# Intermediates of a two-block transformer kernel kept in their PSUM banks, and one bias vector moved

## The chip, the cores and the metric

The kernel runs on one core of a Trainium2 chip. The metric is the time of one execution on the device in microseconds, the median of three runs. The core has five engines with queues of their own: TensorE (PE, matrix products), VectorE (DVE) and ScalarE (ACT) for elementwise work, GpSimd (POOL), and SyncE (SP), which here only issues transfers. An engine takes its instructions in order and waits on semaphores. Operands lie in SBUF; TensorE writes its products into PSUM, eight banks of 128 partitions by 512 float32, which DVE and ACT can read and write.

## What is computed

256 rows of 1024 channels go through two blocks. Shortened:

```python
# block 1
h    = layer_norm(x)
proj = h @ w_in + b_in                  # qa ka va qb kb vb, gates ga gb
y_na, y_swa = neighbourhood(...) @ w_branch_na, windowed(...) @ w_branch_swa
mixed = sigmoid(ga) * y_na + sigmoid(gb) * y_swa
h = layer_norm(alpha * h + mixed @ w_out + b_out)
u = square(relu(h @ w_ff1 + b_ff1))
h = layer_norm(alpha * h + u @ w_ff2 + b_ff2)
# block 2, two layers: pooling mixer, then windowed attention
for layer in range(2):
    m = mixer(rms_norm(x))
    x = x + rms_norm(m, mix_post_g)
    c = conv3(rms_norm(x) @ w_in) + conv_b          # causal, depthwise
    gate, val = split(c)
    x = x + rms_norm((gelu(gate) * val) @ w_out, ffn_post_g)
```

## The kernel before

The 256 rows are two tiles `t` of 128. Every product is carried in a rounded high part and a low part of both operands: `hi*hi + hi*lo + lo*hi`, three matmuls each. Activations are split by ScalarE (high part: a rounding copy) and VectorE (low part: source minus high part); `split_out` (L337) does it for `oh/ol`, `uh/ul`, `ah/al`.

Weights stream in slices of 512 KB. SyncE issues the transfer into `wraw`, ScalarE writes `whi` (L131), VectorE or GpSimd writes `wlo` (L141, function `low`, whose `eng` says which). A slice's next transfer waits until `wlo` is done. `W.pump(n, eng)` prepares slices, `W.take` hands one to TensorE. All of it stands in program order on the engines' queues, without a planner: code order is the order of the work.

PSUM banks come in two rotations of four, `bank_a` and `bank_b`. Units of two output halves (`unit_a`, L371) compute 128 columns by 256 rows per half into a `bank_a`; `epi(m, o)` is what is done with half `m`, and what it returns runs after the slices of that step are pumped. `Tm` is used where the second row tile is late: `run(t)` computes transposed rows, `finish(u, epi)` transposes them back. `Acc` holds the four `bank_b` of a 256x1024 sum; `acc.tail` finishes tile 0 first, so that its norm runs beside the products of tile 1.

The places that the change touches:

- Branch sums, L762 to L779. Four units; per half: gate times branch plus the other branch's product (L770, L772, VectorE), high part (L775, ScalarE), low part (L777, VectorE). Behind each half a slice's `wlo` goes to VectorE (m = 0) or GpSimd (m = 1).
- First norms, `post_ln` (L793): residual sum, statistics, centring (L279), output (L284), on VectorE. Tile 0 runs inside `acc.tail`, tile 1 after it, beside `tm.run(0)`.
- Between `to_fm(h1[1])` and `tm.run(1)`: two VectorE instructions (L907) that turn `h1` into `alpha*h1 + bff2`. `bff2` is a 512 KB broadcast transfer on GpSimd's queue (`vec`, L217).
- Feed-forward: units 3 to 15, each followed by two slices of the second product. Its norms are `a_stats`, `a_centre`, `a_norm`.
- Mixer, L1030 on: the residual product (`resid_g`, L327), sums of squares on ScalarE (`sq_half`, L302), `resid_add` (L331). A product `junk` tile in SBUF joins the two.
- Gated convolution (`conv_ffn`, L1074): per unit half a ScalarE read of the bank (L1085) and two taps on VectorE (L1086, L1088); with m = 1 gelu (L1092, ScalarE), gate product (L1093, VectorE), split. Units 0 to 2 are finished from `Tm` into `bank_b` between the first three of units 3 to 21; while u < 6 GpSimd takes the `wlo` of the pump.

## Time and profile before

| what | value |
|---|---|
| runs | 896.19, 897.50, 894.68 us; median 896.19 |
| profiled execution | 895.49 us, of which span 893.7 us |
| mean granted TensorE clock | 0.984 |
| TensorE busy | 847.2 us (95% of the span) |
| VectorE, ScalarE, GpSimd busy | 630.2 us (71%), 492.2 us (55%), 238.3 us (27%) |
| chain that ended last | PE 66%, DVE 14%, issue 6%, ACT 6%, DMA 5%, POOL 2% |

The profile is of one execution. TensorE is busy in all but some tens of microseconds, so the places that count are those where it stands still and those where its matmuls are spaced wider than elsewhere. A row of a timeline gives the start in microseconds, the duration, the engine, the line of the kernel, the operation, what is written and read, and in brackets the idle time before it with the instruction that ended it. Overlapping starts are the engine's pipeline. For TensorE the distance from one start to the next is the pace, not the printed duration.

### The profile page before, as it was taken

The page shows a single profiled execution, that of the slowest core. Times are in us where ns is not written, and L with a number is a line of the kernel's source. Part 1 is how long each engine was busy: PE and PEld are TensorE (multiplying, and loading weights), DVE is VectorE, ACT ScalarE, POOL GpSimd, SP SyncE. Part 2 cuts the span into 40 slices and gives each one's busy share as a digit, 9 for nine tenths or more (in the row PEclk, how much of TensorE's full clock was granted, in tenths as well). Part 3 has the DMA queues.
Part 4 walks back from the last instruction along what each step waited for, and adds up shares of the span by engine and source line. Part 5 has one row for each costly group of instructions (what it writes and reads, how often), then busy time and mean ns, then how long its engine had stood idle before and what let it go on. Part 6 is the DMA issues. An engine that isn't in the chain of part 4 may idle for free.

```text
span 893.7 us, 15200 instructions
## 1 busy us (share of the span) xinstructions
PE 847.2 (95%) x5872; PEld 764.6 (86%) x5872; DVE 630.2 (71%) x1019; ACT 492.2 (55%) x905; POOL 238.3 (27%) x196
## 2 busy tenths in 40 slices
PE   6999999889899999998999999999999899999997
PEld 5988899768798999788989999988776899999995
DVE  5466754877747755777689877765796678977772
ACT  4555755433535655444666555465786466655551
POOL 4161040323999000343240000046721224000000
PEclk9999999989899999998999999999999999999999
DMA  8683354337635865523447656544152354765531
GB/s 316 201 276 117 134 189 140 120 104 237 224 102 184 278 246 189 184 100 118 165 124 253 217 185 213 179 129 130 59 198 99 142 189 149 261 227 186 179 133 47
DMA packets 43897, 154.61 MB, mean 173 GB/s; under 512 B 5009, under 2 KB 5905, under 8 KB 43826
## 3 DMA queue, kind: packets, MB, share of 16 engines
q1 hardware_dynamic: 41616, 146.90, 48.5%
q0 software_dynamic: 1632, 5.93, 2.1%
q8 instruction: 46, 0.75, 0.3%
q10 hardware_dynamic: 578, 0.82, 0.3%
q14 instruction: 25, 0.20, 0.1%
HBM read 152.58 MB, written 1.05 MB: 172 GB/s over the span
## 4 chain that ended last, share of the span: by engine, by line
PE 66%; DVE 14%; issue 6%; ACT 6%; DMA 5%; POOL 2%; DVEq 0%; POOLq 0%; SPq 0%; ACTq 0%
PE bank_a L369 35%; PE bank_b L369 23%; DVE wlo L141 4%; DMA wraw<-wts_dram 4%; PE bank_a L424 3%; ACT whi L131 2%; DVE p L1262 1%; DVE p L698 1%; ACT p L1274 1%; PE bank_a L720 1%; POOL wlo L141 1%; PE bank_b L709 1%; DVE X L331 1%; DMA v<-bvec_dram 1%; PE bank_b L657 1%
## 5 line engine op out<-in xcount | busy, mean ns | idle before, releaser
L141 DVE TENSOR_TENSOR wlo<-wraw,whi 128x1024 fp32r<-128x1024 f32 x225 | 287.1, 1304 | 78.9 <-ACT whi L131 73.3
L369 PE MATMUL bank_a<-xh,whi 128*128 128x256 f32 x1056 | 297.3, 282 | 4.1 <-DVE cv L1088 3.9
L369 PE MATMUL bank_a<-xh,wlo 128*128 128x256 f32 x1056 | 294.3, 279 | 0.7 <-DVE wlo L141 0.5
L369 PE MATMUL bank_a<-xl,whi 128*128 128x256 f32 x1056 | 294.1, 278 | 0.0
L131 ACT ACTIVATE whi<-wraw 128x1024 fp32r<-128x1024 f32 x261 | 265.5, 1050 | 41.3 <-DMA wraw<-wts_dram 35.0
L369 PEld LDWEIGHTS bank_a<-xh,whi 128*128 128x128 f32 x1056 | 200.0, 189 | 9.2 <-ACT whi L131 4.6
L369 PEld LDWEIGHTS bank_a<-xl,whi 128*128 128x128 f32 x1056 | 200.1, 189 | 1.8
L369 PEld LDWEIGHTS bank_a<-xh,wlo 128*128 128x128 f32 x1056 | 200.0, 189 | 1.3 <-DVE wlo L141 1.0
L141 POOL TENSOR_TENSOR wlo<-wraw,whi 128x1024 fp32r<-128x1024 f32 x36 | 93.6, 2617 | 173.2 <-ACT whi L131 74.8
L1085 ACT ACTIVATE cv<-bank_a,cols 128x256 f32<-128x256 f32 x76 | 41.9, 559 | 78.5 <-PE bank_a L369 78.5
L266 POOL TENSOR_TENSOR rstd<-ve,neghalf 128x1 f32<-128x1 f32 x22 | 13.5, 612 | 232.1 <-DVE ve L307 189.8
L369 PE MATMUL bank_b<-wlo,ah 128*128 128x512 f32 x176 | 69.3, 394 | 0.0
L369 PE MATMUL bank_b<-whi,al 128*128 128x512 f32 x176 | 69.0, 392 | 0.0
L369 PE MATMUL bank_b<-whi,ah 128*128 128x512 f32 x176 | 68.5, 389 | 0.0
L1086 DVE SCALAR_TENSOR_TENSOR cv<-bank_a,cols,cv 128x255 f32<-128x255 f32 x76 | 36.5, 481 | 44.5 <-ACT cv L1085 44.3
L869 POOL TENSOR_SCALAR wraw<-wraw,cols 128x256 f32<-128x256 f32 x28 | 29.5, 1074 | 122.9 <-DVE cv L1086 117.4
L369 PE MATMUL bank_b<-whi,uh 128*128 128x512 f32 x128 | 51.3, 401 | 4.4 <-ACT uh L338 4.4
L369 PE MATMUL bank_b<-whi,ul 128*128 128x512 f32 x128 | 51.4, 402 | 1.7 <-DVE ul L339 1.7
L369 PE MATMUL bank_b<-wlo,uh 128*128 128x512 f32 x128 | 51.2, 400 | 0.0
L369 PEld LDWEIGHTS bank_b<-wlo,ah 128*128 128x128 f32 x176 | 33.1, 188 | 6.6
L1088 DVE SCALAR_TENSOR_TENSOR cv<-bank_a,cols,cv 128x254 f32<-128x254 f32 x76 | 36.6, 482 | 2.7
L369 PEld LDWEIGHTS bank_b<-whi,al 128*128 128x128 f32 x176 | 33.0, 188 | 6.3
(200 smaller groups left out, 1365.8 us busy)
## 6 DMA issues: line engine op xcount, KB each, us to landing
wraw<-wts_dram SPq DMA_DIRECT2D x268, 512.0 KB, 4.4
v<-bvec_dram POOLq DMA_DIRECT2D x10, 512.0 KB, 5.9
v<-bvec_dram SPq DMA_DIRECT2D x4, 512.0 KB, 6.8
nab<-nab_dram SPq DMA_DIRECT2D x4, 384.0 KB, 6.2
poolA<-const_dram POOLq DMA_DIRECT2D x1, 544.0 KB, 6.4
scr<-x_dram SPq DMA_DIRECT2D x2, 256.0 KB, 3.3
scr<-x_dram SPq DMA_DIRECT2D x1, 512.0 KB, 10.1
out_dram<-X SPq DMA_DIRECT2D x2, 256.0 KB, 2.1
```

The costliest lines, as they stand in the source:

```text
L131: self.nc.scalar.activation(out=hi, in_=r, func=AF.Copy)
L141: (eng or self.nc.vector).tensor_tensor(out=lo, in0=r, in1=hi.bitcast(F32), op=ALU.subtract)
L266: nc.gpsimd.tensor_tensor(out=r, in0=v, in1=neghalf, op=ALU.pow)
L331: nc.vector.scalar_tensor_tensor(out=x[:, s], in0=junk[:, s], scalar=r, in1=x[:, s], op0=ALU.mult, op1=ALU.add)
L369: nc.tensor.matmul(o, lhsT=l, rhs=r, start=start and i == 0, stop=stop and i == 2)
L424: nc.tensor.matmul(o[:, :256], lhsT=self.kx(k)[b][:, t * P:(t + 1) * P], rhs=self.cs[u][k // 4][a][:, k % 4, :], start=i == 0 and k == 0, ...
L657: nc.tensor.matmul(s[e][:, j * T:(j + 1) * T], lhsT=q[r, j * P:(j + 1) * P], rhs=k[r, :], start=True, stop=True)
L698: nc.vector.tensor_scalar(out=d, in0=d, scalar1=rc[:, e, j:j + 1], scalar2=None, op0=ALU.mult)
L869: nc.gpsimd.tensor_scalar(out=d, in0=d, scalar1=g, scalar2=None, op0=ALU.mult)
L1085: nc.scalar.activation(out=v, in_=o[:, :T], func=AF.Identity, scale=col(c + 2), bias=col(c + 3))
L1086: nc.vector.scalar_tensor_tensor(out=v[:, 1:T], in0=o[:, 0:T - 1], scalar=col(c + 1), in1=v[:, 1:T], op0=ALU.mult, op1=ALU.add)
L1088: nc.vector.scalar_tensor_tensor(out=v[:, 2:T], in0=o[:, 0:T - 2], scalar=col(c), in1=v[:, 2:T], op0=ALU.mult, op1=ALU.add)
```

## The change

Sums, centred rows, residual products and gated products are written back into the PSUM bank that they were read from, and no longer to SBUF tiles. With that the branch sums' low part is put off by one half (`mix_low`), since the bank holds its source. The mixer's product of half 0 stands behind the two sums of squares, which read the same bank. Gelu writes into the bank of half m = 1 (columns 256 to 511, which the matmuls leave free), the gate product is written there too, and the split reads it from there; the built program lets gelu wait for the second tap of half 1, where it waited for that of half 0 before, since both touch that bank, and the bank comes free with the low part `al`. The transfer of `bff2` and its two VectorE instructions move into the feed-forward, after units 12 and 13. No instruction is added or taken out. The renumbered lines of the changed kernel: L777 becomes L778, L907 becomes L924, L1092 and L1093 become L1097 and L1098.

```diff
@@ -275,20 +275,19 @@
         def ln_centre(y, mr, g, q):
-            s = HALF[q]
-            nc.vector.scalar_tensor_tensor(out=y[:, s], in0=y[:, s], scalar=mr[0], in1=g[:, s],
+            nc.vector.scalar_tensor_tensor(out=y[q], in0=y[q], scalar=mr[0], in1=g[:, HALF[q]],
                                            op0=ALU.subtract, op1=ALU.mult)
 
         def ln_out(y, mr, b, h, q):
             s = HALF[q]
-            nc.vector.scalar_tensor_tensor(out=h[:, s], in0=y[:, s], scalar=mr[1], in1=b[:, s],
+            nc.vector.scalar_tensor_tensor(out=h[:, s], in0=y[q], scalar=mr[1], in1=b[:, s],
                                            op0=ALU.mult, op1=ALU.add)
 
-        def ln_stats(y, st, q, add=None, resid=None):
-            s = HALF[q]
-            if add is not None:
-                nc.vector.tensor_tensor(out=y[:, s], in0=add[q], in1=resid[:, s], op=ALU.add)
-            nc.vector.bn_stats(out=st[:, q, :], in_=y[:, s])
+        def ln_stats(y, st, q, resid=None):
+
+            if resid is not None:
+                nc.vector.tensor_tensor(out=y[q], in0=y[q], in1=resid[:, HALF[q]], op=ALU.add)
+            nc.vector.bn_stats(out=st[:, q, :], in_=y[q])
 
...
@@ -322,13 +321,13 @@
 
-        def resid_g(halves, g, junk, q):
+        def resid_g(halves, g, q):
+
+            nc.vector.tensor_tensor(out=halves[q], in0=halves[q], in1=g[:, HALF[q]], op=ALU.mult)
+
+        def resid_add(r, x, halves, q):
             s = HALF[q]
-            nc.vector.tensor_tensor(out=junk[:, s], in0=halves[q], in1=g[:, s], op=ALU.mult)
-
-        def resid_add(r, x, junk, q):
-            s = HALF[q]
-            nc.vector.scalar_tensor_tensor(out=x[:, s], in0=junk[:, s], scalar=r, in1=x[:, s],
+            nc.vector.scalar_tensor_tensor(out=x[:, s], in0=halves[q], scalar=r, in1=x[:, s],
                                            op0=ALU.mult, op1=ALU.add)
...
@@ -767,19 +766,23 @@
                 g, z = gate["gb", i], gate["ga", i]
-                nc.vector.scalar_tensor_tensor(out=g, in0=g, scalar=1.0, in1=o[:, :T], op0=ALU.add, op1=ALU.mult)
-                s = rot(apool, [P, T], F32, "mix", "mix", 2)
-                nc.vector.tensor_tensor(out=s, in0=g, in1=z, op=ALU.add)
+                s = o[:, :T]
+                nc.vector.scalar_tensor_tensor(out=s, in0=g, scalar=1.0, in1=s, op0=ALU.add, op1=ALU.mult)
+                nc.vector.tensor_tensor(out=s, in0=s, in1=z, op=ALU.add)
                 hi = rot(gpool, [P, T], F32R, "ga", "mixh", 8)
                 lo = rot(gpool, [P, T], F32R, "gb", "mixl", 8)
                 nc.scalar.activation(out=hi, in_=s, func=AF.Copy, scale=0.5)
                 mixed[i] = (hi, lo)
-                return [lambda: nc.vector.scalar_tensor_tensor(out=lo, in0=s, scalar=0.5, in1=hi.bitcast(F32),
-                                                               op0=ALU.mult, op1=ALU.subtract)]
+                if i:
+                    mix_low.pop()()
+                mix_low.append(lambda: nc.vector.scalar_tensor_tensor(
+                    out=lo, in0=s, scalar=0.5, in1=hi.bitcast(F32), op0=ALU.mult, op1=ALU.subtract))
             return epi
 
+        mix_low = []
         for u in range(4):
             unit_a(lambda k: att[4 + k], swa_epi(u), 4, ahead=1)
+        mix_low.pop()()
 
...
@@ -793,8 +796,8 @@
             for q in range(2):
-                ln_stats(y, st, q, acc.b[t], y)
-            layer_norm(y, ln_rstd(st), g, b, h)
+                ln_stats(acc.b[t], st, q, y)
+            layer_norm(acc.b[t], ln_rstd(st), g, b, h)
 
...
@@ -898,19 +901,17 @@
         pscale = vec(V_PSCALE)
-        bff2 = vec(V_BFF2)
         g2 = vec(V_G2)
         b2 = vec(V_B2)
         tm.run(0)
         to_fm(h1[1], xT1, 1)
-        for t in range(2):
-            nc.vector.scalar_tensor_tensor(out=h1[t], in0=h1[t], scalar=ALPHA, in1=bff2, op0=ALU.mult, op1=ALU.add)
         tm.run(1)
...
         nc.gpsimd.dma_start(out=poolA.rearrange("p a c -> p (a c)"), in_=const_in[:, K_POOL:K_POOL + N_POOL])
+        bff2 = vec(V_BFF2)
         mixpost0 = vec(V_MIXPOST0, None, late, "bx", 1)
...
@@ -919,6 +920,9 @@
             unit_a(kx, ff1_epi(u))
+            if u in (12, 13):
+                nc.vector.scalar_tensor_tensor(out=h1[u - 12], in0=h1[u - 12], scalar=ALPHA, in1=bff2, op0=ALU.mult,
+                                               op1=ALU.add)
             for k in (2 * (u - 3), 2 * (u - 3) + 1):
...
@@ -932,18 +936,18 @@
                 st2[t] = small([P, 2, 6], "bst")
-            ln_stats(h1[t], st2[t], q, acc.b[t], h1[t])
+            ln_stats(acc.b[t], st2[t], q, h1[t])
 
         def a_centre(t):
             mr2[t] = ln_rstd(st2[t])
             for q in range(2):
-                ln_centre(h1[t], mr2[t], g2, q)
+                ln_centre(acc.b[t], mr2[t], g2, q)
 
...
             for q in range(2):
-                ln_out(h1[t], mr2[t], b2, X[t], q)
+                ln_out(acc.b[t], mr2[t], b2, X[t], q)
                 sq_half(X[t][:, HALF[q]], junk, ss2[t], q)
...
@@ -1014,11 +1018,11 @@
                 if q == 0:
-                    resid_g(halves, gpost, junk, q)
+                    resid_g(halves, gpost, q)
             r = rms_rstd(ss)
-            resid_g(halves, gpost, junk, 1)
+            resid_g(halves, gpost, 1)
             for q in range(2):
-                resid_add(r, X[t], junk, q)
+                resid_add(r, X[t], halves, q)
 
...
@@ -1032,22 +1036,22 @@
         for q in range(2):
-            ln_out(h1[1], mr2[1], b2, X[1], q)
+            ln_out(acc.b[1], mr2[1], b2, X[1], q)
         for q in range(2):
             sq_half(X[1][:, HALF[q]], j1, ss2[1], q)
         nc.scalar.activation(out=cb, in_=fb[1][:, :P], func=AF.Copy)
-        resid_g(accp.b[0], mixpost0, j0, 0)
         for q in range(2):
             sq_half(accp.b[0][q], j0, ss0, q, 1)
+        resid_g(accp.b[0], mixpost0, 0)
         lows = W.highs(2)
         r1 = rms_rstd(ss2[1])
         a_scale(1, r1)
         r0 = rms_rstd(ss0)
-        resid_g(accp.b[0], mixpost0, j0, 1)
+        resid_g(accp.b[0], mixpost0, 1)
         fb = pool_fm(1, cb)
         lows[0](nc.gpsimd)
         for q in range(2):
-            resid_add(r0, X[0], j0, q)
+            resid_add(r0, X[0], accp.b[0], q)
         fm_split(fb, dT, 1, (0,))
...
@@ -1089,12 +1093,13 @@
                     if m == 1:
-                        nc.scalar.activation(out=got[0], in_=got[0], func=AF.Gelu_apprx_tanh)
-                        nc.vector.tensor_tensor(out=v, in0=v, in1=got[0], op=ALU.mult)
+                        y = o[:, T:2 * T]
+                        nc.scalar.activation(out=y, in_=got[0], func=AF.Gelu_apprx_tanh)
+                        nc.vector.tensor_tensor(out=y, in0=v, in1=y, op=ALU.mult)
                         hi = rot(fp, [P, T], F32R, "ah", "ah", 8)
                         lo = rot(fp, [P, T], F32R, "al", "al", 8)
                         a_t[u] = (hi, lo)
-                        return [lambda: split_out(v, hi, lo)]
+                        return [lambda: split_out(y, hi, lo)]
                 return epi
```

VectorE's queue in the first two halves of the branch sums, before; `gb` and `ga` are the gate tiles in SBUF, `bank_a` a PSUM bank, `mix` the SBUF tile of the sum:

```order
L770 SCALAR_TENSOR_TENSOR gb<-gb,bank_a 128x256
L772 TENSOR_TENSOR mix<-gb,ga 128x256
L141 TENSOR_TENSOR wlo<-wraw,whi 128x1024
L777 SCALAR_TENSOR_TENSOR mixl<-mix,mixh 128x256
L770 SCALAR_TENSOR_TENSOR gb<-gb,bank_a 128x256
L772 TENSOR_TENSOR mix<-gb,ga 128x256
L777 SCALAR_TENSOR_TENSOR mixl<-mix,mixh 128x256
```

and in the changed kernel:

```order
L770 SCALAR_TENSOR_TENSOR bank_a<-gb,bank_a 128x256
L771 TENSOR_TENSOR bank_a<-bank_a,ga 128x256
L141 TENSOR_TENSOR wlo<-wraw,whi 128x1024
L770 SCALAR_TENSOR_TENSOR bank_a<-gb,bank_a 128x256
L771 TENSOR_TENSOR bank_a<-bank_a,ga 128x256
L778 SCALAR_TENSOR_TENSOR mixl<-bank_a,mixh 128x256
```

The low part of a half stands behind the sum of the next half; each sum has one operand in PSUM.

VectorE's queue around the first norm of tile 1 and the start of the feed-forward, before; `v_2301` is `bff2`, `ur` the first feed-forward half:

```order
L279 SCALAR_TENSOR_TENSOR scr<-scr,mv,v_1334 128x512 x2
L284 SCALAR_TENSOR_TENSOR scr<-scr,rstd,v_1336 128x512 x2
L339 TENSOR_TENSOR xl<-bank_a,xh 128x4x128 x2
L907 SCALAR_TENSOR_TENSOR scr<-scr,v_2301 128x1024 x2
L141 TENSOR_TENSOR wlo<-wraw,whi 128x1024 x6
L890 TENSOR_TENSOR ur<-ur 128x256
```

in the changed kernel, at the same place:

```order
L278 SCALAR_TENSOR_TENSOR bank_b<-bank_b,mv,v_1334 128x512 x2
L283 SCALAR_TENSOR_TENSOR scr<-bank_b,rstd,v_1336 128x512 x2
L338 TENSOR_TENSOR xl<-bank_a,xh 128x4x128 x2
L141 TENSOR_TENSOR wlo<-wraw,whi 128x1024 x6
L893 TENSOR_TENSOR ur<-ur 128x256
```

and after unit 12 of the feed-forward, where `v_2573` is `bff2`:

```order
L141 TENSOR_TENSOR wlo<-wraw,whi 128x1024 x2
L338 TENSOR_TENSOR ul<-ur,uh 128x256
L924 SCALAR_TENSOR_TENSOR scr<-scr,v_2573 128x1024
L141 TENSOR_TENSOR wlo<-wraw,whi 128x1024 x2
L893 TENSOR_TENSOR ur<-ur 128x256
```

Nothing stands between the transposes' low parts (`xl`) and the six `wlo` any more.

ScalarE's queue at the first finished unit of the first convolution, before:

```order
L1085 ACTIVATE cv<-bank_b,cols 128x256 x2
L1092 ACT_TABLE_LOAD
L1092 ACTIVATE cv<-cv 128x256
L338 ACTIVATE ah<-cv 128x256
L1085 ACTIVATE cv<-bank_a,cols 128x256
L131 ACTIVATE whi<-wraw 128x1024
L1085 ACTIVATE cv<-bank_a,cols 128x256
```

and in the changed kernel:

```order
L1089 ACTIVATE cv<-bank_b,cols 128x256 x2
L1097 ACT_TABLE_LOAD
L1097 ACTIVATE bank_b<-cv 128x256
L337 ACTIVATE ah<-bank_b 128x256
L1089 ACTIVATE cv<-bank_a,cols 128x256
L131 ACTIVATE whi<-wraw 128x1024
L1089 ACTIVATE cv<-bank_a,cols 128x256
```

The order is the same; gelu (L1097) now writes the bank whose first columns the taps of half 1 read, and `ah` reads that bank. The table load stands in front of it as before and takes over its wait.

## Rows read from the trace of the kernel before

**Rows 1.** VectorE (DVE) timeline, branch sums: start, us, engine, line, operation, [idle before, releaser]

```profile
162.22 0.41 DVE L770 SCALAR_TENSOR_TENSOR gb<-gb,bank_a 128x256 f32<-128x256 f32 x1
...
162.66 2.31 DVE L772 TENSOR_TENSOR mix<-gb,ga 128x256 f32<-128x256 f32 x1
...
166.25 0.43 DVE L772 TENSOR_TENSOR mix<-gb,ga 128x256 f32<-128x256 f32 x1
...
179.75 2.01 DVE L777 SCALAR_TENSOR_TENSOR mixl<-mix,mixh 128x256 fp32r<-128x256 f32 x1 [0.48 <-ACT mixh L775]
```

**Rows 2.** GpSimd (POOL) timeline, the same stretch

```profile
162.31 2.39 POOL L141 TENSOR_TENSOR wlo<-wraw,whi 128x1024 fp32r<-128x1024 f32 x1 [32.54 <-DVE mixl L777]
...
179.04 2.44 POOL L141 TENSOR_TENSOR wlo<-wraw,whi 128x1024 fp32r<-128x1024 f32 x1 [2.55 <-ACT whi L131]
```

**Rows 3.** TensorE (PE) timeline, branch sums and the tail of the out-projection

```profile
166.36 0.35 PE L369 MATMUL bank_a<-oh,whi 128*128 128x256 f32 x1 [1.65 <-DVE gb L770]
...
177.84 0.39 PE L369 MATMUL bank_b<-whi,mixl 128*128 128x512 f32 x1
...
178.07 0.40 PE L369 MATMUL bank_b<-wlo,mixh 128*128 128x512 f32 x1
...
179.02 0.50 PE L369 MATMUL bank_b<-whi,mixh 128*128 128x512 f32 x1 [0.55 <-ACT whi L131]
...
181.53 0.49 PE L369 MATMUL bank_b<-wlo,mixh 128*128 128x512 f32 x1 [1.78 <-POOL wlo L141]
...
182.95 0.79 PE L369 MATMUL bank_b<-whi,mixh 128*128 128x512 f32 x1 [0.93 <-ACT whi L131]
...
188.65 0.50 PE L369 MATMUL bank_b<-whi,mixh 128*128 128x512 f32 x1
```

**Rows 4.** VectorE timeline, first norm of the first half of the rows

```profile
194.12 2.90 DVE L284 SCALAR_TENSOR_TENSOR scr<-scr,rstd,v 128x512 f32<-128x512 f32 x1
```

**Rows 5.** TensorE timeline, before the transposes of the second half

```profile
210.09 1.18 PE L348 MATMUL bank_a<-ident,scr 128*128 128x128 f32 x7 [1.36 <-DVE scr L284]
```

**Rows 6.** VectorE timeline, after the first norm

```profile
216.27 2.36 DVE L907 SCALAR_TENSOR_TENSOR scr<-scr,v 128x1024 f32<-128x1024 f32 x2 [3.53 <-DMA v<-bvec_dram]
```

**Rows 7.** ScalarE (ACT) timeline, the same stretch

```profile
215.01 2.00 ACT L131 ACTIVATE whi<-wraw 128x1024 fp32r<-128x1024 f32 x2
```

**Rows 8.** Waits of TensorE from 226 to 232: engine, line, waited for, us, times, longest

```profile
PE bank_b L369 <- ACT uh L338: 4.4, 1, 4.4
```

**Rows 9.** Windows: bounds, length, busy (x instructions) by engine, PEclk, DMA share, GB/s

```profile
231.00:240.00 9.00, 9.00 (x32) 7.20 (x33) 8.52 (x11) 7.02 (x12) 8.42 (x8) 0.69 0.50 150
...
240.00:358.00 118.00, 117.89 (x780) 107.36 (x779) 74.83 (x94) 62.07 (x96) 47.86 (x46) 1.00 0.59 203
...
452.00:582.00 130.00, 130.00 (x945) 122.50 (x944) 102.89 (x153) 75.94 (x120) 8.45 (x4) 0.99 0.59 199
```

**Rows 10.** VectorE timeline, mixer

```profile
396.76 0.68 DVE L327 TENSOR_TENSOR scr<-bank_b,v 128x512 f32<-128x512 f32 x1
...
400.85 3.50 DVE L331 SCALAR_TENSOR_TENSOR X<-scr,rstd,X 128x512 f32<-128x512 f32 x2
```

**Rows 11.** ScalarE timeline, mixer

```profile
399.00 0.20 ACT L302 ACTIVATION_READ_ACCUMULATOR scr<-bank_b 128x1 f32 x1
```

**Rows 12.** TensorE timeline, mixer

```profile
405.01 0.58 PE L369 MATMUL bank_b<-whi,xl 128*128 128x256 f32 x1 [2.27 <-DVE xl L339]
```

**Rows 13.** VectorE timeline, first units of the first convolution, and its loop

```profile
442.59 1.18 DVE L1093 TENSOR_TENSOR cv<-cv 128x256 f32<-128x256 f32 x1
...
444.25 2.06 DVE L339 TENSOR_TENSOR al<-cv,ah 128x256 fp32r<-128x256 f32 x1 [0.48 <-ACT ah L338]
...
452.11 1.15 DVE L1093 TENSOR_TENSOR cv<-cv 128x256 f32<-128x256 f32 x1
...
516.20 0.48 DVE L1086 SCALAR_TENSOR_TENSOR cv<-bank_a,cols,cv 128x255 f32<-128x255 f32 x1 [1.72 <-ACT cv L1085]
```

**Rows 14.** TensorE timeline, first units of the first convolution

```profile
450.74 0.36 PE L369 MATMUL bank_a<-xh,whi 128*128 128x256 f32 x1 [1.86 <-DVE cv L1088]
```

More of the change, by code (lines that the diff above doesn't have):

```diff
@@ L497, in ln0 @@
             for q in range(2):
-                ln_stats(x_t[t], st, q)
+                ln_stats(halved(x_t[t]), st, q)
             mr = ln_rstd(st)
             mid()
-            layer_norm(x_t[t], mr, g0, b0, x_t[t], mid2)
+            layer_norm(halved(x_t[t]), mr, g0, b0, x_t[t], mid2)
         ln0(0, lambda: lows.pop(0)(nc.gpsimd))
@@ L991, in mid_a @@
                 fm_split(fb[0], dT, 0, (q,))
-                ln_centre(h1[1], mr2[1], g2, q)
+                ln_centre(acc.b[1], mr2[1], g2, q)
         ffnpre0 = vec(V_FFNPRE0)
@@ L1067, in model @@
         for q in range(2):
-            resid_g(accp.b[1], mixpost0, j1, q)
+            resid_g(accp.b[1], mixpost0, q)
         for q in range(2):
-            resid_add(r1, X[1], j1, q)
+            resid_add(r1, X[1], accp.b[1], q)
         h0 = pre_rms(1, ffnpre0, j1)
@@ L1135, in l1_chain @@
                 if q == 0:
-                    resid_g(acc.b[t], gpost, j, q)
+                    resid_g(acc.b[t], gpost, q)
             r = rms_rstd(ss)
-            resid_g(acc.b[t], gpost, j, 1)
+            resid_g(acc.b[t], gpost, 1)
             lows = W.highs(2 - t)
             for q in range(2):
-                resid_add(r, X[t], j, q)
+                resid_add(r, X[t], acc.b[t], q)
             ss = small([P, 2], "ss")
```

## Prediction

> **What bounds the kernel now.** I read the page first: TensorE is busy for 95% of the span, so a change on the other engines counts only where TensorE stands still or is paced down. Then I listed TensorE's pauses from its timeline, with what ended each, and looked up in VectorE's and GpSimd's timelines what the releasing engine had done just before. Both long inner loops have no pause worth naming: 117.89 of 118 us and 130 of 130 us are busy [rows 9]. What the change can win or lose lies at the stage borders.
>
> At these borders one pattern returns. Writing `mix` in the branch sums takes 0.43 us, but 2.31 us where it starts while GpSimd works on a `wlo`: it ends at 164.97, GpSimd's at 164.70 [rows 1, 2]. The low part at 179.75 takes 2.01 us and ends at 181.76, beside GpSimd's 179.04 to 181.48 [rows 1, 2]. Both read two SBUF tensors. The instruction at 162.22, one operand in PSUM, starts 0.09 us before GpSimd's and runs 0.41 us across its start undisturbed [rows 1, 2]. The stretched ones elsewhere have the same shape: L284 with 2.90 us [rows 4], L331 with 3.50 for a pair [rows 10], L1093 and L339 with 1.18 and 2.06 [rows 13]. After the change each of these has an operand in PSUM. I therefore cost them at their undisturbed size: 0.43 us for 256 columns, and 0.7 for 512 (1.4 a pair), an estimate from L327, which takes 0.68 with one operand in PSUM [rows 10].
>
> **The change part by part.** Sums are made against the profiled 895.49 us, 0.7 under the median.
>
> *Branch sums and the out-projection.* VectorE loses 2.31 - 0.43 = 1.9 and 2.01 - 0.43 = 1.6 us to the two stretched instructions shown [rows 1], and there are two of each: 7 us. Until the last unit TensorE gains nothing: its first pause of 1.65 us ends with the release of a bank by L770 [rows 3], and in the changed kernel the bank is held past the sum and the copy to the low part one half later, so what VectorE saves is spent on the longer hold. I take zero, with ends of -1.7 and +1.5. After it TensorE waits for weight slices: 0.55 + 1.78 + 0.93 = 3.26 us before 179.02, 181.53 and 182.95 [rows 3]. These came late because VectorE's low parts stood in the way: the `whi` at 182 had its SBUF slot from a `mix` tile and GpSimd's last `wlo` began at 179.04. Without the stretches and that slot GpSimd's last `wlo` can start up to 7 us earlier, so all three pauses go: 3.3. Behind them TensorE runs slow: from 182.95 to 188.65 twelve matmuls start in 5.70 us, 0.475 each, where just before it was 0.23 (177.84 to 178.07) [rows 3]. That is half the pace, the lower clock level, after the pauses; without them it is 5.70 - 12 x 0.23 = 2.9 us less. Sum: -6.2, ends 0 and -7.9. What is late next is TensorE itself: it has all slices and its pace sets the stage's end.
>
> *First norms.* L284 of tile 0 runs beside the tail and is hidden, but VectorE is free 2.2 us (2.90 - 0.7) earlier for the norm of tile 1, and the transposes at 210.09 that waited 1.36 us for it [rows 4, 5] find it done: -1.3, ends 0 and -1.4.
>
> *`bff2`.* VectorE sat 3.53 us idle for the transfer and then took 2.36 us for two instructions, ending at 218.63 [rows 6]. Its first `wlo` stood behind them, although the `whi` pair had begun at 215.01, so that the first was there at about 216.1 [rows 7]. All that follows (slice transfers that wait for `wlo`, then `whi`, `wlo`, the first feed-forward half) moves up by 218.6 - 216.1 = 2.5 us at most, and TensorE's wait of 4.4 us [rows 8] shrinks to 2.0: -2.4. The slower clock after it, 0.69 over 9 us [rows 9], would give back up to 9 x 0.31 = 2.8 more if the pause fell short enough; I take none. Ends 0 and -5.2. GpSimd's queue issues the transfer later, behind `poolA`; the rest of that queue moves up by one issue. The two instructions land in the feed-forward, where VectorE is busy 74.8 of 118 us [rows 9]: 2.4 us hidden, and 2.4 if that cover were gone.
>
> *Norms after the feed-forward, the last chains, the norm at the very start.* The same instructions at the same place in the queue, no stretched one in them: 0.
>
> *Mixer.* The pair at L331 takes 3.50 us and falls to 1.4: -2.1. Against it, the product that ran at 396.76 must now wait for ScalarE's square of the same bank, over at 399.2 [rows 10, 11]. Behind it on VectorE stand `ve`, the scaling of the pool matrix and with that the second pooling product; they come 2.3 us later, but of this only the part before 400.85 reaches the pair: followed through, its end and the `xl` that TensorE waited 2.27 us for [rows 12] come 0.6 to 0.7 us earlier. -0.7, ends -3.5 and +1.5.
>
> *Gated convolution, once per layer.* Before unit 6 the units repeat every 452.11 - 442.59 = 9.5 us [rows 13], which is VectorE's chain, and TensorE is let go by L1088 after 1.86 us [rows 14]. Of these 9.5 the stretches are 0.75 + 1.63 = 2.4. New is that gelu waits for half 1's taps instead of running beside them. A hand-over to ScalarE and back shows 0.48 us of idle before L339 [rows 13]; it now comes once more in the finished unit (+0.5) and in the other with a `whi` copy of 1.0 us between (+1.1; half of the pair's 2.00 in [rows 7]). Cycle: 9.5 - 2.4 + 1.6 = 8.7. The gain of 0.8 is used up by the first gelu, whose table load begins 0.9 later, so unit 6 starts about as before (+0.2). But bank m = 1 is free only after `al`, some 2.6 us after the tap that freed it before. I find +0.95 for unit 6's half 1 and +0.55 for unit 7's. +1.7 a layer, +3.4 for both; ends -3.5 and +3 a layer. In the loop behind, VectorE waits 1.72 us for ScalarE in every unit [rows 13], 102.9 and 75.9 of 130 us are busy [rows 9] (16 units, 8.1 us each), and a bank is wanted again two units later: gelu's 0.5 us is hidden there.
>
> *PSUM as a destination.* No row shows VectorE or ScalarE writing a bank. The nearest, an instruction with one operand read there, takes 0.41 against 0.43 us [rows 1]. Ends are -0.02 and +0.75 us an instruction (1.18 - 0.43, the stretched L1093); I take 0. In the chain before unit 6 two a unit count, 6 units a layer, so +0.1 us each would be +2.4 in all.
>
> [...]
>
> Sum: -6.2 - 1.3 - 2.4 - 0.7 + 3.4 = -7.2, that is 888.3 on the profiled run and 889.0 on the median; I say 888.5.
>
> **The rivals.**
> 1. *More clock.* Pauses at 226, 402 and 448 that shrink also shorten the slow stretches after them (2.8 us at 231 alone). The 9 us at 0.69 [rows 9] speak for it, that pauses remain there against it. With two or three such returns 5 us more: 883, down to 879.
> 2. *No change.* The weight slices, not the stretches, set the pace: SyncE's transfers and ScalarE's `whi` arrive where they did, so of the 6.2 only the clock part or nothing comes, and the convolutions cost 3.4: 895.5 - 1.3 - 2.4 - 0.7 + 3.4 + 0 to -3 = 891.5 to 894.5. For it: two of the three pauses end with `whi` [rows 3]. Against: VectorE had waiting copies in front of it all the time.
> 3. *Slower: the held banks at the convolution's start.* `al` of units 4 to 6 falls behind the pumped `wlo` on VectorE (1.2 us each, half of the 2.36 pair is the nearest row [rows 6]), and TensorE finds bank m = 1 taken at three halves in both layers. It decides once the six waits sum to over 10.6 us, the gain elsewhere: 1.8 us each. At three slices each (3.6 us) it is 6 x 3.6 - 10.6 = +11: 906. For it: the hold grows in just this place, and the chain there is VectorE's. Against: GpSimd takes the `wlo` until unit 6.
>
> **How the numbers follow.** Chances: the forecast (884 to 891) 0.56, more clock 0.17, no change 0.17, slower 0.10. A measurement of this kernel tells 0.3% (2.7 us) from no change, so faster is below 893.5. Of the rival "no change" about a third still falls below that and is counted as faster, and 0.02 of the slower one lies within 0.3%: faster 0.78, same 0.14, slower 0.08. The range reaches from 879, most of the clock rival, to 895.5, most of the third case.
>
> **What the next profile would show.** Branch sums and L284, L331, L1093, L339 at their undisturbed size beside GpSimd's `wlo`; the three pauses of 3.26 us and the twelve slow matmuls gone; the pause before the first feed-forward product near 2.0; VectorE's L327 (mixer) starting after ScalarE's square; in the convolutions a cycle of 8.7 us and short new waits of TensorE for `al`. I am wrong if the instructions stay stretched with an operand in PSUM, if a bank as a destination costs over 0.3 us, or if TensorE waits for `al` in the loop.

## The result and the profile after

The changed kernel takes 884.88 us (median of four runs, 882.88 to 889.15) against 896.73 of the kernel before on the same chip; the ratio is 0.9875 with an interval of 0.9844 to 0.9906. The time is 1.25% shorter; the forecast was 888.5 in a range of 879.0 to 895.5. The profiled execution took 883.26 us, span 881.5, mean granted clock 0.990 (before 895.49, 893.7 and 0.984).

Both kernels issue the same 5872 matmuls in the same order, so the lead of the changed one can be read by setting the start of the n-th matmul in one TensorE timeline beside the n-th in the other:

| up to | before, us | after, us | lead won in this stretch | forecast |
|---|---|---|---|---|
| last unit of the branch sums | 168.53 | 168.63 | 0.1 (from 0.2 behind) | 0 |
| tail of the out-projection, same matmul | 188.99 | 181.95 | 7.1 | 6.2 |
| transposes after the first norm | 210.09 | 201.40 | 1.7 | 1.3 |
| end of the feed-forward loop | 371.76 | 358.77 | 4.3 | 2.4 |
| mixer | 420.51 | 406.52 | 1.0 | 0.7 |
| first convolution | 598.73 | 584.57 | 0.2 | -1.7 |
| its last norm and the attention | 725.91 | 714.42 | -2.7 | 0 |
| second convolution and the end | 887.09 | 874.86 | 0.7 | -1.7 |

A trace is of one execution, so a term has to recur before it can be put down to the change. The tail (7.1) and the first norms (1.7) recur within 0.1 us in every trace of the experiments below that has the same code there. The feed-forward's term lies between 3.8 and 4.7 us in the seven traces with the bias moved and all the rest of the change in front of it. The mixer's lies between -0.5 and +1.8 us in five traces with the same mixer, and the stretch with the last norm and the attention loses 0.6 to 2.4 us even in the three experiments that leave its code as it was before. These two rows can't be read off the table alone; the account further down comes back to them.

VectorE in the branch sums of the changed kernel (start, us, engine, line, operation), then GpSimd in the same stretch:

```profile
162.51 0.43 DVE L771 TENSOR_TENSOR bank_a<-bank_a,ga 128x256 f32<-128x256 f32 x1
...
163.97 0.41 DVE L778 SCALAR_TENSOR_TENSOR mixl<-bank_a,mixh 128x256 fp32r<-128x256 f32 x1
...
169.67 0.43 DVE L771 TENSOR_TENSOR bank_a<-bank_a,ga 128x256 f32<-128x256 f32 x1
170.01 0.41 DVE L778 SCALAR_TENSOR_TENSOR mixl<-bank_a,mixh 128x256 fp32r<-128x256 f32 x1
```

```profile
162.45 2.39 POOL L141 TENSOR_TENSOR wlo<-wraw,whi 128x1024 fp32r<-128x1024 f32 x1 [32.52 <-ACT whi L131]
...
169.30 4.79 POOL L141 TENSOR_TENSOR wlo<-wraw,whi 128x1024 fp32r<-128x1024 f32 x2 [1.14 <-DVE mixl L778]
```

The sum at 162.51 and the low part at 163.97 run at 0.43 and 0.41 us while GpSimd's `wlo` of 162.45 is at work; the ones at 169.67 and 170.01 lie in its pair from 169.30. Those of before took 2.31 and 2.01 [rows 1]. GpSimd's last `wlo` ends at 174.1, not at 181.5 [rows 2].

TensorE of the changed kernel in the stretch of [rows 3]:

```profile
163.32 0.38 PE L368 MATMUL bank_a<-oh,whi 128*128 128x256 f32 x1 [1.28 <-DVE mixl L778]
...
167.11 0.39 PE L368 MATMUL bank_a<-oh,whi 128*128 128x256 f32 x1 [0.70 <-DVE mixl L778]
...
178.29 0.39 PE L368 MATMUL bank_b<-whi,mixh 128*128 128x512 f32 x1
...
178.98 0.39 PE L368 MATMUL bank_b<-whi,mixh 128*128 128x512 f32 x1
...
181.95 0.39 PE L368 MATMUL bank_b<-whi,mixl 128*128 128x512 f32 x1
```

The last of these is the matmul that the kernel before starts at 188.99:

```profile
188.99 0.39 PE L369 MATMUL bank_b<-whi,mixl 128*128 128x512 f32 x1
```

Before, TensorE waited twice for a bank, 2.2 us in all; two such pauses remain (1.28 and 0.70 us). The three before `whi` and `wlo` are gone, and from 178.98 to 181.95 thirteen matmuls start 0.23 us apart. The windows of the changed kernel (bounds, length, busy by engine, PEclk, DMA share, GB/s) show the full clock (1.00) there and after the first feed-forward product, and a lower one in the mixer (0.54) and after the attention (0.72):

```profile
182.00:189.00 7.00, 7.00 (x32) 5.77 (x31) 4.91 (x9) 2.19 (x3) 2.92 (x2) 1.00 0.01 4
218.00:227.00 9.00, 9.00 (x52) 7.72 (x53) 8.00 (x11) 7.39 (x12) 8.34 (x9) 1.00 0.46 162
388.00:394.00 6.00, 5.68 (x28) 5.68 (x29) 3.69 (x8) 3.86 (x8) 3.42 (x3) 0.54 0.24 69
686.00:692.00 6.00, 5.84 (x36) 5.84 (x37) 4.92 (x9) 3.57 (x11) 0.65 (x2) 0.72 0.66 253
```

The first norm's output and TensorE's transposes after it, without the pause of [rows 5]:

```profile
187.09 1.40 DVE L283 SCALAR_TENSOR_TENSOR scr<-bank_b,rstd,v 128x512 f32<-128x512 f32 x2
```

```profile
201.40 1.14 PE L347 MATMUL bank_a<-ident,scr 128*128 128x128 f32 x8
```

The pair of L283 takes 1.40 us, beside GpSimd's `wlo` of 186.45; its one instruction in [rows 4] took 2.90.

Around the bias, VectorE's first `wlo`, and TensorE's first two waits for the feed-forward's halves:

```profile
207.25 2.42 DVE L141 TENSOR_TENSOR wlo<-wraw,whi 128x1024 fp32r<-128x1024 f32 x2 [3.30 <-ACT whi L131]
```

```profile
217.99 0.51 PE L368 MATMUL bank_b<-whi,uh 128*128 128x512 f32 x1 [0.39 <-ACT uh L337]
...
231.01 0.50 PE L368 MATMUL bank_b<-whi,uh 128*128 128x512 f32 x1 [0.91 <-ACT uh L337]
```

The `wlo` no longer stands behind anything but its `whi`, and the pause of 4.4 us [rows 8] is 0.39; the next product waits 0.91, which it did not before.

The mixer, VectorE and then TensorE:

```profile
386.35 0.70 DVE L326 TENSOR_TENSOR bank_b<-bank_b,v 128x512 f32<-128x512 f32 x1 [2.42 <-ACT scr L301]
...
387.77 0.49 DVE L956 TENSOR_SCALAR poolA<-poolA,rstd 128x512 f32<-128x512 f32 x1 [0.66 <-POOL rstd L266]
...
389.06 1.41 DVE L330 SCALAR_TENSOR_TENSOR X<-bank_b,rstd,X 128x512 f32<-128x512 f32 x2
```

```profile
388.32 2.08 PE L977 MATMUL bank_a<-poolA,X 128*128 128x128 f32 x8 [2.89 <-DVE poolA L956]
```

The pair of L330 takes 1.41 us, not 3.50 [rows 10]. But the first residual product starts only when ScalarE's square is done, 2.42 us of idle, the scaling of the pool matrix behind it comes at 387.77, and TensorE waits 2.89 us for it where it waited 0.67.

The start of the convolution, two successive units on VectorE, and TensorE's waits around both starts (engine, line, waited for, us in total, times, longest):

```profile
429.97 0.43 DVE L1098 TENSOR_TENSOR bank_a<-cv,bank_a 128x256 f32<-128x256 f32 x1 [0.52 <-ACT bank_a L1097]
431.21 0.42 DVE L338 TENSOR_TENSOR al<-bank_a,ah 128x256 fp32r<-128x256 f32 x1 [0.82 <-ACT ah L337]
...
438.36 0.43 DVE L1098 TENSOR_TENSOR bank_a<-cv,bank_a 128x256 f32<-128x256 f32 x1 [0.52 <-ACT bank_a L1097]
439.60 0.42 DVE L338 TENSOR_TENSOR al<-bank_a,ah 128x256 fp32r<-128x256 f32 x1 [0.82 <-ACT ah L337]
```

```profile
PE bank_a L368 <- DVE cv L1092: 1.9, 1, 1.9
```

```profile
PE bank_a L368 <- DVE cv L1092: 1.4, 1, 1.4
PE bank_a L368 <- DVE al L338: 0.8, 2, 0.4
```

The cycle is 8.39 us (429.97 to 438.36); before it was 9.52 [rows 13]. The product takes 0.43 and the low part 0.42 us, after 0.52 us of idle for gelu and 0.82 for `ah`.

### The profile page after: what moved, and what is told of

Same layout as the page of the kernel before. It is cut to its first block, busy times and chain, and to the rows that moved or that the text cites. A ratio compares the mean times of both kernels' runs of the same rounds, so it can differ in the third digit from the quotient of the medians.

```text
span 881.5 us, 15123 instructions
## 1 busy us (share of the span) xinstructions
PE 842.5 (96%) x5872; PEld 761.3 (86%) x5872; DVE 605.8 (69%) x1019; ACT 490.8 (56%) x905; POOL 237.3 (27%) x196
## 3 DMA queue, kind: packets, MB, share of 16 engines
q1 hardware_dynamic: 41616, 146.90, 48.8%
## 4 chain that ended last, share of the span: by engine, by line
PE 67%; DVE 14%; ACT 7%; issue 5%; DMA 4%; POOL 2%; SPq 0%; DVEq 0%; POOLq 0%; ACTq 0%
PE bank_a L368 34%; PE bank_b L368 22%; PE bank_a L423 6%; DVE wlo L141 5%; DMA wraw<-wts_dram 4%; ACT whi L131 3%; DVE p L697 1%; DVE p L1267 1%; ACT p L1279 1%; DVE cv L1092 1%; PE bank_a L719 1%; DVE cv L1090 1%; PE bank_b L708 1%; ACT cv L1089 1%; PE bank_b L656 1%
## 5 line engine op out<-in xcount | busy, mean ns | idle before, releaser
L141 DVE TENSOR_TENSOR wlo<-wraw,whi 128x1024 fp32r<-128x1024 f32 x225 | 290.5, 1318 | 99.1 <-ACT whi L131 98.1
L1097 ACT ACTIVATE bank_a<-cv 128x256 f32<-128x256 f32 x38 | 14.8, 388 | 62.8 <-DVE cv L1092 62.8
```

What stands on the lines that cost most here:

```text
L141: (eng or self.nc.vector).tensor_tensor(out=lo, in0=r, in1=hi.bitcast(F32), op=ALU.subtract)
L1097: nc.scalar.activation(out=y, in_=got[0], func=AF.Gelu_apprx_tanh)
```

## Experiments

Each ratio is to the kernel before, run beside the experiment on the same chip (medians 897.28, 895.64 and 895.30 us). The experiments ran on three chips and at other times than the result, so two of them are compared by their ratios, and small differences between their medians mean little.

**The bias alone.** The kernel before with the transfer and the two instructions moved:

```diff
-        bff2 = vec(V_BFF2)            # before tm.run(0)
-        for t in range(2): ... h1[t] = ALPHA * h1[t] + bff2
+        bff2 = vec(V_BFF2)            # behind poolA
+            if u in (12, 13): ... h1[u - 12] = ALPHA * h1[u - 12] + bff2
```

> The kernel before with nothing but the bias moved into the feed-forward. Theory (the bias's transfer and its two VectorE instructions held up the weight slices): the pause before the first feed-forward product, 4.43 us, shrinks to about 1.2 and the slow matmuls after it go, so 4 us less of span by the middle of the feed-forward and a time of 891 to 894 (0.4% less). Rival (the pause is set by the slices' transfers alone): the pause stays at 4 us or more, time within 1 us of the kernel before.

Measured: 891.64 us against 897.28, ratio 0.9948 (0.9928 to 0.9968). VectorE's first `wlo` and TensorE's first product:

```profile
216.18 2.56 DVE L141 TENSOR_TENSOR wlo<-wraw,whi 128x1024 fp32r<-128x1024 f32 x2 [3.35 <-ACT whi L131]
```

```profile
227.51 0.50 PE L369 MATMUL bank_b<-whi,uh 128*128 128x512 f32 x1 [0.97 <-ACT uh L338]
```

The pause is 0.97 us. The lead jumps by 3.4 us there, grows to 5.8 through the matmuls that no longer run slow, falls to 4.4 at the next unit's product, where TensorE now waits for the feed-forward's half, and is 3.5 at the end of the loop: what the clock gave was waited away again. The bias alone is worth half a per cent.

**The branch sums alone.** The kernel before with the changed `swa_epi`, the part that computes the branch sums, and nothing else.

> The kernel before with the branch sums alone in PSUM. Theory (two-input SBUF instructions are held by GpSimd, one input in PSUM frees them): all eight sums at 0.43 us, the three pauses of 0.55, 1.78 and 0.93 us and the twelve slow matmuls gone, 6 to 7 us less by the end of the out-projection, time about 889 to 891. L284 in the first norm may stay stretched beside GpSimd. Rival (the gain at that border needs the first norms in PSUM as well): under 3 us less.

Measured: 889.09 us against 897.28, ratio 0.992 (0.9889 to 0.9952), six runs from 885.3 to 894.6. In its trace all eight sums take 0.43 us, and the lead is 7.1 us at the matmul of 188.99, the same as in the changed kernel, and still 7.1 at the transposes of 210.09: the 1.7 us there belong to the first norm. The profiled execution was the slowest of its six and had lost most of that lead by the end. 2.9 us of it went between the matmuls that the kernel before starts at 752 and 868, evenly, without a wait and at a granted clock of 1.00; no run here shows why. I read only the early stages from it.

**Which input counts.** The changed kernel with the gate product back in SBUF, so that the sum reads two SBUF tensors and writes the bank:

```diff
-  scalar_tensor_tensor(out=s, in0=g, scalar=1.0, in1=s, ...)
-  tensor_tensor(out=s, in0=s, in1=z, op=ALU.add)
+  scalar_tensor_tensor(out=g, in0=g, scalar=1.0, in1=s, ...)
+  tensor_tensor(out=s, in0=g, in1=z, op=ALU.add)
```

> The changed kernel with one difference in the branch sums: the gate product goes back to its SBUF tile, and the sum reads two SBUF tensors (gate product and gate a) and writes the bank. Theory (it is the second SBUF input that GpSimd holds): the sums that start beside a GpSimd weight low part take 2 us or more again, though their destination is PSUM, and the low parts (bank and one SBUF tensor) stay at 0.41 us. Rival (a destination in PSUM is what frees the instruction): all sums at 0.43 us.

Measured: one run, 887.40 us. VectorE, then GpSimd:

```profile
163.38 2.58 DVE L771 TENSOR_TENSOR bank_a<-gb,ga 128x256 f32<-128x256 f32 x1
165.87 0.41 DVE L778 SCALAR_TENSOR_TENSOR mixl<-bank_a,mixh 128x256 fp32r<-128x256 f32 x1
...
166.64 0.43 DVE L771 TENSOR_TENSOR bank_a<-gb,ga 128x256 f32<-128x256 f32 x1
...
168.94 2.35 DVE L771 TENSOR_TENSOR bank_a<-gb,ga 128x256 f32<-128x256 f32 x1
```

```profile
163.33 2.34 POOL L141 TENSOR_TENSOR wlo<-wraw,whi 128x1024 fp32r<-128x1024 f32 x1 [32.50 <-ACT whi L131]
168.61 2.38 POOL L141 TENSOR_TENSOR wlo<-wraw,whi 128x1024 fp32r<-128x1024 f32 x1 [2.95 <-DVE wlo L141]
```

The sums that fall beside GpSimd's `wlo` take 2.58 and 2.35 us and end 0.3 us after it ends, though they write a bank; the one at 166.64, clear of it, takes 0.43. The low part at 165.87, bank and SBUF, stays at 0.41, like the others. So the second SBUF input makes the difference, and the destination does not. At the matmul of 181.95 this kernel is 4.7 us behind the changed one; it is still 2.3 us ahead of the kernel before, and its low parts are not stretched.

**No GpSimd.** The kernel before with `low((nc.vector, nc.gpsimd)[m])` replaced by `low(nc.vector)`.

> The kernel before, everything in SBUF, with the four weight low parts of the branch sums that GpSimd did given to VectorE. Theory (the stretch is GpSimd's doing, not that of the tiles' place): no sum and no low part of the branch sums over 0.45 us; VectorE does four slices more (4 x 1.22 = 4.9 us) and loses 7 us of stretch, so the tail starts with fewer pauses, about 4 to 7 us less by its end. Rival (the instructions are stretched by something else, say transfers into SBUF): they stay at 2.0 to 2.3 us.

Measured: one run, 892.08 us. Two of VectorE's instructions, at 0.43 and 0.42 us; none of the sixteen took more:

```profile
163.56 0.43 DVE L772 TENSOR_TENSOR mix<-gb,ga 128x256 f32<-128x256 f32 x1
...
177.48 0.42 DVE L777 SCALAR_TENSOR_TENSOR mixl<-mix,mixh 128x256 fp32r<-128x256 f32 x1
```

The tail is 6.0 us earlier at the matmul of 188.99, with the order of the queue as it was before: moving the low parts by one half is not needed for most of the gain. Giving GpSimd four slices cost VectorE more (four stretched instructions, two sums 1.9 us and two low parts 1.6 us over their undisturbed size, 7.0 in all) than they took from it (4 x 1.22 = 4.9 us). This and the run before it tie the stretch to GpSimd's work from both sides.

**The convolution back in SBUF.** The changed kernel with gelu and the product of before.

> The changed kernel with the gated product back in SBUF, as before the change. My forecast said that the product in PSUM costs 3.4 us over both layers, so this would be 3.4 us faster than the changed kernel (881 to 882). The trace of the changed kernel says that it costs nothing: two new waits of 0.43 and 0.35 us in layer 1, none in layer 0, a cycle of 8.4 instead of 9.5 us. By the trace: L1093 and L339 stretched again, unit cycle 9.5 us, pauses of 1.9 and 2.1 us, and a time within 1.5 us of the changed kernel.

Measured: 884.21 us, ratio 0.9855 (0.983 to 0.9879): the changed kernel's time. VectorE, and TensorE's wait in layer 1:

```profile
430.00 1.18 DVE L1097 TENSOR_TENSOR cv<-cv 128x256 f32<-128x256 f32 x1
431.66 2.06 DVE L338 TENSOR_TENSOR al<-cv,ah 128x256 fp32r<-128x256 f32 x1 [0.48 <-ACT ah L337]
...
439.51 1.18 DVE L1097 TENSOR_TENSOR cv<-cv 128x256 f32<-128x256 f32 x1
```

```profile
PE bank_a L368 <- DVE cv L1092: 1.9, 1, 1.9
```

The stretches are back and the cycle is 9.51 us. Across the first convolution this kernel wins 0.2 us on the changed one, in the second and what follows it loses 0.7. My term of 3.4 us is refuted; the two kernels differ by about half a microsecond over both layers, in the other direction.

**Gelu without its new wait.** The second tap of half 1 writes the bank, gelu stays in SBUF:

```diff
+                    y = o[:, T:2 * T] if m else v
+                    if m:
+                        nc.vector.tensor_copy(out=y[:, 0:2], in_=v[:, 0:2])
-                    scalar_tensor_tensor(out=v[:, 2:T], in0=o[:, 0:T - 2], ...)
+                    scalar_tensor_tensor(out=y[:, 2:T], in0=o[:, 0:T - 2], ...)
...
-                        activation(out=y, in_=got[0], func=AF.Gelu_apprx_tanh)
-                        tensor_tensor(out=y, in0=v, in1=y, op=ALU.mult)
+                        activation(out=got[0], in_=got[0], func=AF.Gelu_apprx_tanh)
+                        tensor_tensor(out=y, in0=y, in1=got[0], op=ALU.mult)
```

> The changed kernel, but in the convolution the second tap of half 1 writes the bank (its first two columns by a small copy), gelu stays in SBUF and so waits for half 0's tap alone, and the product reads the bank and the SBUF gelu. One SBUF input everywhere, no wait of gelu for half 1. Theory (gelu's wait is what keeps the cycle at 8.4 us): a cycle of about 7.5 us, the pauses before unit 6 (1.9 and 1.4 us) and the two of 0.4 us in layer 1 shrink, 1 to 3 us less, 882 to 884. Rival (the extra copy, 76 of them, and the clock eat it): same as the changed kernel, 884 to 886.

Measured: 876.99 us, ratio 0.9789 (0.9762 to 0.9816), 0.9%, or some 8 us, below the changed kernel's 0.9875, with intervals that don't meet, and more than expected. Two successive units on VectorE:

```profile
426.97 0.16 DVE L1094 COPY bank_a<-cv 128x2 f32<-128x2 f32 x1
...
427.76 0.43 DVE L1100 TENSOR_TENSOR bank_a<-bank_a,cv 128x256 f32<-128x256 f32 x1
...
435.37 0.43 DVE L1100 TENSOR_TENSOR bank_a<-bank_a,cv 128x256 f32<-128x256 f32 x1
```

The product follows the tap without idle, the copy costs 0.16 us, the cycle is 7.61 us, and the trace shows no wait of TensorE for a bank at either start. Across each convolution 3.3 and 3.0 us are won on the changed kernel. So the change's new wait costs 3 us a layer. Against the run with the convolution back in SBUF, which has the stretches and not the wait, 3.1 and 3.8 us are won: the stretches that the change takes away pay about as much as its wait costs.

**The mixer's product later.** The changed kernel with `resid_g(accp.b[0], mixpost0, 0)` behind `a_scale(1, r1)`.

> The changed kernel with the mixer's first residual product moved behind the scaling of the pool matrix on VectorE. Theory (its new wait for ScalarE's square holds the scaling behind it): the pause before the second pooling product falls from 2.89 to about 0.7 us, and the later part of the mixer comes 1 to 2 us earlier; time 883 to 884. Rival (the pair of residual sums is late anyway): the pause of 2.2 us turns up again before the first product that needs the split, time unchanged.

Measured: 882.87 us, ratio 0.9841 (0.9816 to 0.9866), no clear difference from the changed kernel. TensorE's waits in the mixer:

```profile
PE bank_a L347 <- DVE scr L321: 1.5, 1, 1.5
PE bank_b L368 <- ACT xh L337: 0.9, 1, 0.9
PE bank_b L368 <- DVE xl L338: 0.9, 2, 0.6
PE bank_a L977 <- DVE poolA L956: 0.7, 1, 0.7
```

The pause of 2.89 us is 0.7 again; 0.9 and 0.3 of it come back one step later as waits for the split (`xh`, `xl`), and 0.2 at the transposes. The mixer ends 1.0 us earlier, but 0.4 of that lead was there before it began. The rest need not be the edit's: the mean granted clock in this mixer was 0.96, against 0.93 in the changed kernel, and the run without gelu's wait, whose mixer is that of the changed kernel, also had 0.96 and took 46.95 us for the same matmuls where this one took 47.09. That fits the rival; a gain of the edit is not shown.

**Both.**

> Both edits that look better than the changed kernel: gelu in SBUF with the tap in the bank, and the mixer's first residual product behind the scaling of the pool matrix. If they add up: about 1 us from the mixer and 1 to 3 from the convolutions, 880 to 883. If the gain is lost to waits further on: 883 to 885.

Measured: 874.89 us, ratio 0.9767 (0.9736 to 0.9797), below both expectations. It has the lowest median of the versions tried, 1.1%, or some 10 us, below the changed kernel; against the gelu edit alone the intervals overlap, so a gain from the mixer's edit is not shown here either.

**The transfer put back.** The changed kernel with a 512 KB transfer of the bias, into a tile that nobody reads, behind `pscale`.

> The changed kernel with one more transfer of 512 KB (the bias, into a tile that nobody reads) at the place on GpSimd's queue where it stood before; the two VectorE instructions stay in the feed-forward. It splits the bias's gain. Theory (I had forecast 2.4 us for the two instructions and found 3.4 to 4.2; the rest is the transfer, which delays the weight slices): the weight copy before the first feed-forward half comes 1 to 1.5 us later and the pause before the first feed-forward product grows from 0.39 to about 1.8 us. Rival (the rest came from elsewhere, the transfer is free): the pause stays at 0.4 us.

Measured: 884.32 us, ratio 0.9876 (0.985 to 0.9902).

```profile
217.26 0.51 PE L368 MATMUL bank_b<-whi,uh 128*128 128x512 f32 x1 [0.24 <-ACT uh L337]
```

The pause is 0.24 us, not 1.8. The theory falls: this trace shows no cost of the transfer's traffic there. What is left of the bias's cost is VectorE's wait for it and the two instructions, in front of the slices.

## Why the prediction was right, and where not

The time lies in the range and the direction is right; the lead won is 12.4 us by the trace where 7.2 were forecast. That the total came out this near is partly luck: the convolutions' term was wrong by 4.3 us, the tail and the bias were too small by 0.9 and 1.9, and against these stand 2.7 us that were lost where nothing was forecast.

*What bounds the kernel:* right. Both loops stayed dense (104.90 of 105 us busy from 240 to 345, 130.00 of 130 from 440 to 570), and what was won lies at the borders named; 2.7 us were lost at others.

*The stretch:* right, and now shown from three sides: the sums took 0.43 us with one input in PSUM, 2.58 and 2.35 with two SBUF inputs and a PSUM destination, and 0.42 or 0.43 without GpSimd.

*Branch sums and tail:* right; 7.1 against 6.2. The three pauses went, and so did the slow matmuls: the granted clock was 0.50 from 182.95 to 188.65 before, and is 1.00 from 182 to 189 after. The zero for the units before it holds as well.

*First norms:* right, 1.7 against 1.3, and the run with the sums alone shows that it is a term of its own.

*`bff2`:* the mechanism was right, the term mis-sized: 2.4 forecast, 4.3 in the changed kernel, 3.5 by the same point when moved alone (3.6 won in that stretch). The first `wlo` moved up by 2.4 (218.55 to 216.18 in the run of the bias alone), as worked out; the pause shrank by 3.5. The slower matmuls after it, for which I took nothing, returned 2.3 more, and all of that was given back in the first part of the loop, 1.4 of it at the next unit's product, where TensorE now waits for both parts of the feed-forward's half, so that the shorter pause alone makes the term. The missing 1.1 of the pause arises between the first `wlo` and the first feed-forward half, and the traces show where: the second slice's transfer took 5.7 us from issue to landing in the kernel before (issued at 221.1), 5.0 in the run of the bias alone (218.8) and 4.5 in the changed kernel (209.7), and the last `wlo` before the first half took 1.47, 1.23 and 1.22 us. In the kernel before, the third transfer was issued 1.1 us behind the second, since four `wlo` ran in a row; in the other two 1.5 and 1.6 us behind. That this is what lengthened the transfer I suspect, and no run tests it; the run with the transfer put back excludes only the bias's own traffic.

*Mixer:* 1.0 against 0.7; the new wait for the square and the delay of 2.2 us of the second pooling product were as described. The size needs the clock beside it, since mixers with the same code differ by more than the term. Length of the stretch from the matmul of 371.76 to that of 420.51, by the mean granted clock in it:

| granted clock | mixer of before, us | changed mixer, us |
|---|---|---|
| 0.96 | 47.7 (bias alone) | 47.0 (without gelu's wait) |
| 0.93 | 48.8 (before) | 47.7 (changed), 47.9 (transfer put back) |
| 0.90 | | 49.0 (two SBUF inputs), 49.3 (convolution in SBUF) |
| 0.87 | 50.6 (sums alone), 50.9 (no GpSimd) | |

At the same clock the changed mixer is 0.8 to 1.0 us shorter, which bears out the term; the clock itself moves the stretch by 2 to 3 us between kernels with the same code.

*Convolution:* this is the step that failed; the slower convolutions of the forecast (+1.7 us a layer) did not come, and TensorE's start of unit 6 kept its lead. But of the waits for `al` (0.95 and 0.55 a layer) none appears in layer 0 and two of about 0.4 in layer 1. Two things show in rows. The cycle was forecast at 8.7 us and is 8.4, over three cycles before unit 6. And TensorE ran slower there after its pause: the granted clock from 438 to 444 was 0.73,

```profile
438.00:444.00 6.00, 6.00 (x41) 5.96 (x40) 3.72 (x9) 3.92 (x9) 3.19 (x2) 0.73 0.43 128
```

so that it came to unit 6's second half only at about 440.8, when `al` of unit 4 (439.60 and 0.42 us) was done at 440.0; at full pace, by estimate 2.8 us after 436.6 (24 matmuls at the 0.12 us of 436.8 to 437.6), it would have waited 0.6. Two runs with the same convolution bear this out: with two SBUF inputs and with the transfer put back, the pause before unit 6 was 1.7 and 1.6 us, the granted clock in the 6 us after it 1.00, and there TensorE did wait for `al`, 0.53 us in each; the run with the mixer's product later had 0.73 and no such wait. With the transfer put back:

```profile
PE bank_a L368 <- DVE al L338: 0.5, 1, 0.5
```

So one of the two waits of the forecast is real at the full clock, at about half its size (0.53 against 0.95); the other appears in no trace of layer 0. The run with the convolution back in SBUF shows the balance, the one without gelu's new wait shows that two large terms, 3 us a layer each, cancel in it. What the text missed altogether is that the wait itself was avoidable.

*Last norms:* forecast 0. The trace after loses 2.7 us between the two convolutions, 0.8 of it in one place, where three of the seven traces with this code lose it: `rstd` of the last norm waits on GpSimd's queue behind four scalings of a weight slice.

```profile
577.57 3.63 POOL L872 TENSOR_SCALAR wraw<-wraw,cols 128x256 f32<-128x256 f32 x4 [2.51 <-DMA wraw<-wts_dram]
581.16 0.57 POOL L266 TENSOR_TENSOR rstd<-ve,neghalf 128x1 f32<-128x1 f32 x1
```

The scalings began 2.5 us after GpSimd ran out of work, when their slice had landed; the kernel before has the same 2.5 us, but there the norm came later, and its `rstd` stood 0.8 us behind `ve` instead of 2.1. Another 1.5 us go at 686, where the clock is 0.72 over the 6 us after a pause of 2.47 us; before it was 1.00 after 2.53. That part is not the change's doing: the sums alone and the kernel without GpSimd's slices, whose code at this place is that of before, also had 0.72 there, and they lost 1.6 and 2.4 us in the whole stretch. At the full clock there the bias alone lost 0.6 in the stretch, and the run with two SBUF inputs, which has the change's code, 1.2: little is left that the change could have cost, and none of it is shown.

*PSUM as a destination:* zero was right. Sum, product and low part take 0.41 to 0.43 us, and gelu into the bank 0.39 against 0.41 into SBUF. As a source the bank showed no cost either: the low part took 0.41 to 0.42 us from it and 0.42 to 0.43 from SBUF.

*The rivals:* "more clock" happened after the bias (2.3 us) but was waited away again in the loop, so it is not why the time came out below the forecast; the convolutions, the pause before the feed-forward and the tail are. "No change" did not happen. Of "held banks" the waits of about half a microsecond appeared, not the long ones.

## What to carry to other kernels

Where VectorE and GpSimd share a stage, look for VectorE instructions with two SBUF tensor inputs that take several times their usual length and end with GpSimd's (here 2.31 us against 0.43 for a sum, 2.01 against 0.43 for a low part): give them one operand in PSUM, or give GpSimd's work away; here either brought them back to 0.43 or less. When a product moves into a bank, look at every engine that touches that bank: here the built program let gelu, which writes columns 256 to 511, wait for the tap that reads the columns before them, and choosing another operand for the bank took that wait away and won 3.3 and 3.0 us in the two convolutions. An instruction that waits for a transfer does not only cost its own time; on an in-order queue it delays the copies that start the next transfers (here, with the bias alone moved, the first copy came at 216.18 instead of 218.55, a transfer behind it was issued at 218.8 instead of 221.1, and the pause shrank from 4.4 to 0.97 us). The slow matmuls that went away behind that shorter pause gave 2.3 us, which was waited away again in the loop: count such a term only where nothing waits right after it.

## What was not expected of the hardware

TensorE's pace after a pause did not follow from the pause's length alone. After 4.4 us of waiting it ran at a granted clock of 0.69 over the next 9 us [rows 9], after 0.39 at 1.00, but in the mixer after 2.89 at 0.54. The pause that ends near 686 in the changed kernel is in all eleven traces. The granted clock over the 6 us after it was 1.00 in three of them, behind pauses of 2.4 to 2.7 us (before, bias alone, two SBUF inputs), 0.72 to 0.76 in seven, behind 2.4 to 3.6 us, and 0.50 in one, behind 3.6 us (without gelu's wait). The order of the work before it is nearly the same in all; what decides is not shown. Such stretches move a stage by 1 to 3 us between kernels that share its code, as in the mixer, and the scatter of the small terms has to be read with the granted clock beside it. The clock does not explain all of it: the sums alone lost 2.9 us in the second convolution at a granted clock of 1.00.
